# The 24 merge-gate tiles of a hybrid backbone layer, computed in pairs by Strassen's scheme after the RNN

## The chip, the cores and the metric

The kernel runs on one core of a Trainium2 chip. The metric is the device time of one execution in microseconds (us). The engines are TensorE (PE: matmuls; PEld: weight loads), VectorE (DVE), ScalarE (ACT), GpSimd (POOL) and SyncE (SP, which issues the DMAs). The kernel before takes 3270.88 us, the median of 3 runs (3266.74 to 3272.98).

## The reference

The reference runs two layers of a backbone over 1152 tokens, 1024 latent ones and 128 of a prompt, that share weights. D_MODEL is 1024. Cut to what matters here, one layer is:

```python
h = rmsnorm(x, g_norm) * (1 + scale) + shift            # scale, shift from a modulation matmul
parts = split(h @ w_in)                                  # x_rnn, g_rnn, c_q, c_kv, ..., merge_logits (3 x 1024)
xc = centred_conv(x_rnn, conv_w, conv_b)                 # 4 taps
r, i = sigmoid(xc @ w_a), sigmoid(xc @ w_i)              # block diagonal, 8 blocks of 128; forward and backward
a = exp(8 * r * log_sigmoid(lam))
u = sqrt(1 - a * a) * i * xc
y_rnn = scan(a, u) + reverse_scan(a, u)                  # h_t = a_t h_(t-1) + u_t
m = sigmoid(merge_logits)                                # three gates of 1024 channels per token
u = m0 * ((y_rnn * silu(g_rnn)) @ w_br_rnn) + m1 * (y_mla_gated @ w_br_mla) + m2 * (y_swa_gated @ w_br_swa)
x = x + gate * (u @ w_out)
```

The two attention branches (mla and swa) lie between the RNN and the last line and are not touched by the change. The columns of `w_in` that make `merge_logits` are 24 tiles of 128.

## The kernel before

All values are kept transposed, features on the 128 partitions and tokens along the free axis; the 1152 tokens are cut into 3 chunks of 384. Precision comes from splitting each operand into a high and a low half (`split`: ACT casts the high half, DVE or POOL subtracts it from the source) and issuing three matmuls per product of two 128-blocks (`mm3`: high by high, high by low, low by high). `H` holds the split normed input of a layer, one tile per chunk and half, 8 blocks of 128 features each. A weight tile of `w_in` is 128 output features by 1024 inputs: it is loaded by SP into one of three raw buffers (tag "wr"), split by ACT and POOL (`wload`) and used for three pieces of 24 matmuls, one per chunk.

The order of PE's instructions is the order of the program (`manual_schedule`); the order on the other engines is chosen by a scheduler from priorities and a model of time.

The first half of a layer is one block of code. `rnn_units(ft)` makes the 8 feature tiles of the RNN, each of 18 pieces: three x pieces (their evacuation into `xpad`; behind the last of them the convolution on DVE, L559 and L562, and the split into `xh` and `xl`), three g pieces (evacuated into `gsil`), and 12 gate pieces of 3 matmuls each, whose sigmoid is L587. Behind the last gate piece `scan()` runs on ACT, DVE and POOL (L600 to L622); it ends with the product in `gsil`, which SP stores as `yr` (L623). The buffers of a feature tile (`xpad`, `xc`, `xh`, `xl`, `gsil`, `r0`, `i0`, `r1`, `i1`, pool `rp`) exist once; `scan()` takes the buffers of `xh` and `xl` for its temporaries.

Between the RNN's pieces PE runs filler pieces from a list: eight feature-major tiles (silu gates of the two attention branches, 3 pieces each), five token-major tiles (9 pieces each) and the 24 merge-gate tiles (3 pieces each), 141 pieces. How many run behind which of the 18 pieces stands in

```python
RF = (0,) * 5 + (2,) + (1,) * 11 + (2,)
```

and `late_norm`, in the first feature tile of a layer, runs 4 more. Every third filler piece is followed by a step of the modulation matmuls (in layer 0 those left of layer 0 and all of layer 1; in layer 1 there are none). What is left of the list runs after the RNN, while four of the eight `yr` tiles are loaded back and split into the RNN's own buffers. A merge-gate piece is evacuated by a sigmoid on ACT (L728) and stored to `sg` in DRAM.

Then the merge of the RNN branch starts (`merge`, first unit `wide`, L855): it multiplies `w_br_rnn` with the 8 split `yr` tiles, takes the gates from `sg`, and interleaves the preparation of the mla branch. The other four `yr` tiles are loaded at its head. The rest of the layer (mla, swa, their merges, the output projection and the norm that makes the next layer's `H`) follows.

Of the kernel before, what the change touches and what calls it, by code (L numbers as in the profile page):

```python
# [9 lines left out]
F32 = mybir.dt.float32  # L10
# [16 lines left out]
RW = 1156  # L27
CTX = 1027
EPS = 1e-6
BIG = float(2.0 ** 100)  # L30
# [161 lines left out]
def _backbone(ctx, tc, nc, a, depth):  # L192
# [11 lines left out]
    def f(x):  # L204
        return x.bitcast(F32)
# [200 lines left out]

    def make_h(sp, hp, xt, rs, c, L, nm):
        hh = hp.tile([P, KT, CH], F32R, tag=f"h{c}", name=f"hh{nm}")
        hl = hp.tile([P, KT, CH], F32R, tag=f"l{c}", name=f"hl{nm}")
# [12 lines left out]
        return hh, hl  # L422

    hst = ExitStack()
    hp = pool("hp0", side="right", stack=hst)
    xp2 = pool("xp0", side="right", stack=hst)
    H = []
    with ExitStack() as ist:
# [32 lines left out]
        with tc.manual_schedule(engines={E.PE, E.Activation, E.DVE, E.Pool}):  # L461
# [29 lines left out]
            for c in range(2):  # L491
                H.append(make_h(sp, hp, [xts[c][:, k] for k in range(KT)], None, c, L, f"i{c}"))
        mod_units = mod_units[16:]

    for l in range(depth):
# [32 lines left out]

        rpst = ExitStack()
        with ExitStack() as rst:  # L530
            rp = pool(f"rnn{l}", stack=rpst)
            fp = pool(f"fw{l}", bufs=2, stack=rst)
            ep = pool(f"ev{l}", bufs=2, stack=rst)
            tp = pool(f"tm{l}", stack=rst)
            mdp = pool(f"md{l}", bufs=1, stack=rst)
            psr = pool(f"psr{l}", bufs=3, space=PSUM, stack=rst)
            rows = tp.tile([P, R_SINK], F32, name=f"rows{l}")
# [197 lines left out]
            mod_units = mod_units + more  # L735
            fill = []
            for i in range(5):
                if i == 4:
                    fill.append(tm_unit(i, tms[i]))
                if i < 4:  # L740
                    fill.append(in_unit("b", 16 + i, ev_silu(gm_d[i]), fp))
                    fill.append(in_unit("b", 20 + i, ev_silu(gs_d[:, i]), fp))
                    fill.append(tm_unit(i, tms[i]))
                if i == 3:
                    fill.append(in_unit("b", 24, ev_sig(sg_d[0]), fp))
            for m in range(1, 24):
                fill.append(in_unit("b", 24 + m, ev_sig(sg_d[m]), fp))

# [8 lines left out]
            def filler():  # L757
                if not G and count[0] == 4:
                    G.append(stream(mod_units))
                if next(F, G) is G:  # L760
                    return False
                count[0] += 1
                if count[0] % 3 == 0 and G:
                    next(G[0], None)
                return True

# [10 lines left out]
            def late_norm():  # L777
# [23 lines left out]
                for k in range(KT):  # L801
                    nc.vector.tensor_tensor(out=x2[k], in0=x2[k], in1=rs, op=ALU.mult)
                H.append(make_h(None, hp, x2, None, 2, L, f"i2_{l}"))
                filler()
# [3 lines left out]
            with tc.manual_schedule(engines={mybir.EngineType.PE}):  # L808
                for ft in range(8):
                    for _ in steps(ft):  # L810
                        pass
                    if ft == 1 and decay:
                        decay()
                ys = {}
                for g in range(2):
                    raw = xp2.tile([P, KT, 384], F32, tag="twl", name=f"yrb{l}_{g}").rearrange("p k n -> p (k n)")
                    for j in range(2):
                        k, y = 2 * g + j, raw[:, j * T:(j + 1) * T]
                        ys[k] = [rp.tile([P, T], F32R, tag=t, name=f"y{t}{l}_{k}")
                                 for t in (("r0", "r1"), ("i0", "i1"), ("xc", "xh"), ("xl", "gsil"))[k]]  # L820
# [6 lines left out]
                for _ in R:  # L827
                    pass

        hst.close()  # L830

# [48 lines left out]
        with ExitStack() as ast:  # L880
# [9 lines left out]
            with ExitStack() as yst:  # L890
                yrw = pool(f"yraw{l}", bufs=3, stack=yst)
                with tc.high_priority(offset=1500):
                    for i, k in enumerate((6, 7, 4, 5)):
                        if i < 3:
                            raw = yrw.tile([P, T], F32, tag="yr", name=f"yraw{l}_{k}")
                        else:
                            raw = rp.tile([P, XW], F32, tag="xpad", name=f"yraw{l}_{k}")[:, 0:T]
                        nc.sync.dma_start(out=raw, in_=yr_d[k])
                        split(ys[k][0], ys[k][1], raw, "act", "dve")

# [94 lines left out]

            M = stream(merge(ps6, "b", sp, "rnn", 8, a["w_br_rnn"][l], ys, 0, True, False, None, (0, 1, 2, 3, 6, 7, 4, 5)))
            groups = ([lambda g=g: ck_part(g) for g in range(0, 10, 2)] + [lambda: (kr_load(), [])[1]] +
# [19 lines left out]
            mst.close()  # L1017
            rpst.close()
            pso = pool(f"pso{l}", bufs=1, space=PSUM, stack=ast)
# [624 lines left out]
        xp2 = pool(f"xp{l + 1}", side="right", stack=hst)  # L1644
        UH = [hp.tile([P, KT, CH], F32R, tag=f"h{c}", name=f"uh{l}_{c}") for c in range(NCH)]
        UL = [hp.tile([P, KT, CH], F32R, tag=f"l{c}", name=f"ul{l}_{c}") for c in range(NCH)]
        psn = pool(f"psn{l}", bufs=1, space=PSUM, stack=fst)
# [89 lines left out]
        def cast(c):  # L1737
            rs = rstd_cast(fp, psn, "n", acc[c], f"y{l}_{c}")
            if not last:
                H2[c] = make_h(fp, hp, [xn[c][:, k] for k in range(KT)], rs, c, Ln, f"h{l}_{c}")  # L1740
                return
# [178 lines left out]
```

## Time and profile before

| what | value |
|---|---|
| median of 3 runs | 3270.88 us |
| the profiled execution's own time | 3271.47 us |
| its span (first to last instruction) | 3269.7 us |
| mean granted TensorE clock | 0.992 |
| PE busy | 3169.1 us (97%) |
| DVE, ACT, POOL busy | 1815.7, 1547.4, 1455.6 us (56%, 47%, 45%) |

The profile is of one execution. Busy PE time is made of matmuls whose records overlap, so the time that one matmul takes from its neighbours is read from starts or from counts in a stretch, not from the mean duration in a row. The RNN with its filler lies at about 50 to 902 us for layer 0 and 1660 to 2489 us for layer 1.

### The profile page before, as it was taken

What the parts mean: (1) busy time and instruction counts of PE and PEld (TensorE: products, weight loads), DVE (VectorE), ACT (ScalarE), POOL (GpSimd) and SP (SyncE); (2) the same over time, 40 slices, a digit from 0 to 9 for tenths busy, and PEclk for the clock granted to TensorE, in tenths of its full rate; (3) what the DMA queues carried; (4) which work ended last, traced back from release to release, by engine and by line L of the source; (5) the groups of instructions that cost most, each with busy time, mean ns of one, the idle gap of its engine ahead of it and who ended that gap; (6) DMA issues with size and microseconds to landing.
All of it is one profiled execution on the core that took longest, in us unless ns stands there. A gap on an engine that the chain in (4) does not pass through costs nothing. (4 is left out here: it accounts for less than half of the span.)

```text
span 3269.7 us, 52185 instructions
## 1 busy us (share of the span) xinstructions
PE 3169.1 (97%) x19572; PEld 3039.1 (93%) x19572; DVE 1815.7 (56%) x3253; ACT 1547.4 (47%) x3061; POOL 1455.6 (45%) x1174
## 2 busy tenths in 40 slices
PE   7999999999999999999999999999999999999998
PEld 4999999999999999898989999999999999989998
DVE  5345544322336888987572444433332388898766
ACT  3344444443315777764243433334342277786532
POOL 3655554443313444465374444333322144445643
PEclk9999999999999999999999999999999999999999
DMA  5333333333342102357533222222234400045564
GB/s 213 100 100 103 96 94 109 96 114 96 132 151 69 30 26 51 116 165 236 174 118 100 76 79 79 82 82 79 81 110 145 130 20 25 27 112 154 186 204 134
DMA packets 246652, 351.06 MB, mean 107 GB/s; under 512 B 73216, under 2 KB 200832, under 8 KB 246144
## 3 DMA queue, kind: packets, MB, share of 16 engines
q1 hardware_dynamic: 246400, 347.73, 34.1%
q8 instruction: 154, 2.52, 0.3%
q14 instruction: 98, 0.80, 0.1%
HBM read 248.87 MB, written 98.78 MB: 106 GB/s over the span
## 5 line engine op out<-in xcount | busy, mean ns | idle before, releaser
L239 PE MATMUL in<-hhi,wh_in 128*128 128x384 f32 x1536 | 519.8, 338 | 6.7 <-ACT osg L728 5.1
L239 PE MATMUL in<-hli,wh_in 128*128 128x384 f32 x1536 | 519.4, 338 | 2.2 <-DVE hli L421 2.1
L239 PE MATMUL in<-hhi,wl_in 128*128 128x384 f32 x1536 | 518.3, 337 | 0.0
L215 POOL TENSOR_TENSOR wl_in<-wr_in,wh_in 128x1024 fp32r<-128x1024 f32 x94 | 238.1, 2537 | 320.9 <-ACT wh_in L209 248.6
L239 PEld LDWEIGHTS in<-hhi,wh_in 128*128 128x128 f32 x1536 | 290.0, 189 | 7.6 <-ACT osg L728 5.8
L239 PEld LDWEIGHTS in<-hli,wh_in 128*128 128x128 f32 x1536 | 289.9, 189 | 4.7 <-DVE hli L421 4.7
L239 PEld LDWEIGHTS in<-hhi,wl_in 128*128 128x128 f32 x1536 | 290.0, 189 | 0.0
L239 PE MATMUL in<-hlh,wh_in 128*128 128x384 f32 x768 | 259.2, 337 | 2.3 <-DVE hlh L421 2.2
L239 PE MATMUL in<-hhh,wl_in 128*128 128x384 f32 x768 | 258.7, 337 | 2.1 <-POOL wl_in L215 2.1
L239 PE MATMUL in<-hhh,wh_in 128*128 128x384 f32 x768 | 258.7, 337 | 0.8 <-ACT osg L728 0.8
L1163 POOL TENSOR_SCALAR p<-p,mx 128x1152 f32<-128x1152 f32 x128 | 157.7, 1232 | 200.7 <-DVE mx L1160 124.3
L1214 DVE TENSOR_TENSOR pl<-pt,ph 128x512 fp32r<-128x512 f32 (+1 forms) x320 | 201.5, 637 | 27.9 <-ACT ph L1210 25.1
L1210 ACT CAST ph<-pt 128x512 fp32r<-128x512 f32 (+1 forms) x320 | 170.5, 551 | 91.5 <-PE pt L1203 87.0
L604 DVE SCALAR_TENSOR_TENSOR r<-r,txl 128x1156 f32<-128x1156 f32 x16 | 31.5, 1966 | 315.2 <-ACT r L603 315.2
L1203 PE MATMUL pt<-ident,p 128*128 128x128 f32 x1152 | 171.0, 274 | 9.8 <-DVE kl L1073 4.2
L728 ACT ACTIVATE osg<-in 128x384 f32<-128x384 f32 x144 | 68.9, 488 | 233.4 <-PE in L239 151.2
L1203 PEld LDWEIGHTS pt<-ident,p 128*128 128x128 f32 x1152 | 132.7, 140 | 34.4 <-DVE pl L1214 11.7
L209 ACT CAST wh_in<-wr_in 128x1024 fp32r<-128x1024 f32 x96 | 99.9, 1044 | 123.7 <-PE in L239 85.9
L1228 PE MATMUL o<-ph,v 128*128 128x256 f32 x576 | 153.0, 292 | 0.0
L239 PEld LDWEIGHTS in<-hlh,wh_in 128*128 128x128 f32 x768 | 144.4, 188 | 3.9 <-DVE hlh L421 3.9
L239 PEld LDWEIGHTS in<-hhh,wl_in 128*128 128x128 f32 x768 | 144.6, 188 | 2.4 <-POOL wl_in L215 2.4
L1228 PE MATMUL o<-pl,v 128*128 128x256 f32 x576 | 145.7, 280 | 0.0
(447 smaller groups left out, 9584.1 us busy)
## 6 DMA issues: line engine op xcount, KB each, us to landing
wr_in<-in_w_fm SPq DMA_DIRECT2D x96, 512.0 KB, 3.6
sg<-osg SPq DMA_DIRECT2D x144, 192.0 KB, 1.9
wr_wm<-in_w_mod SPq DMA_DIRECT2D x32, 512.0 KB, 4.1
wr_wo<-in_w_out SPq DMA_DIRECT2D x32, 512.0 KB, 3.7
yr<-gsil SPq DMA_DIRECT2D x16, 576.0 KB, 2.8
msgrnn<-sg SPq DMA_DIRECT2D x48, 192.0 KB, 2.4
u<-msgrnn SPq DMA_DIRECT2D x48, 192.0 KB, 2.6
qr<-qs SPq DMA_DIRECT2D x36, 256.0 KB, 4.0
```

The source lines that it names most:

```text
L209: nc.scalar.copy(out=hi, in_=src)
L215: eng.tensor_tensor(out=lo, in0=src, in1=f(hi), op=ALU.subtract)
L239: nc.tensor.matmul(ps, x, y, start=n == 0, stop=n == last)
L604: nc.vector.scalar_tensor_tensor(out=rr[d], in0=rr[d], scalar=1.0, in1=tt[d], op0=ALU.add, op1=ALU.mult)
L728: nc.scalar.activation(out=o, in_=ps, func=ACT.Sigmoid)
L1163: nc.gpsimd.tensor_scalar(out=pts[i], in0=pts[i], scalar1=mxs[i][:, 5:6], scalar2=1.0, op0=ALU.mult, op1=ALU.mult)
L1203: nc.tensor.transpose(ps[:, w:w + P], pts[q][:, k * P:(k + 1) * P], ident)
L1210: nc.scalar.copy(out=r["h", j][:, 0:width(j)], in_=r["t", j][:, 0:width(j)])
L1214: nc.vector.tensor_tensor(out=r["l", j][:, 0:width(j)], in0=r["t", j][:, 0:width(j)], in1=f(r["h", j][:, 0:width(j)]), op=ALU.subtract)
L1228: nc.tensor.matmul(O[:, 0:256], V[k][:, h % 4, :], x[:, 256 * i:256 * i + 256], start=k == 0 and e == 0, stop=k == 8 and e == 1)
```

## The change

The merge-gate tiles leave the filler list, whose order is written anew (69 pieces). `RF` and `steps` stay. `H` becomes two large tiles (`HB`, high and low), of which the chunks are slices.

After the RNN's pieces the pools of the RNN and the token-major tiles are closed, and three pairs of tiles `T1`, `T2`, `T4` (512 features by 576 tokens, in two halves) are opened in their memory. `H` is read as a 2 x 2 block matrix (`B11` to `B22`, 512 features by 576 tokens). `combine` makes `T1 = B12 - B11`, `T2 = B22 - T1`, `T4 = B21 - T2`, and `B22 - B12` in the place of `B12`. Two merge-gate weight tiles form the other 2 x 2 block matrix. For each of the 12 pairs seven products of 4 x 3 matmuls run over two column pieces (320 and 256), instead of 2 x 24 matmuls over each of three chunks of 384; sums of weight blocks are made on DVE and POOL (`sx`) and each weight block is split anew; sums of products are taken on evacuation by DVE, the sigmoid by ACT on 576 columns. A modulation step may follow a product as it followed a filler piece. At the head of the merge all eight `yr` tiles are loaded into tiles of their own, each raw into the tile of its low half.

```diff
+NH = 576
+SP = ((0, 0, 320), (512, 320, 576))
...
-            fill = []
-            for i in range(5):
-                if i == 4:
-                    fill.append(tm_unit(i, tms[i]))
-                if i < 4:
-                    fill.append(in_unit("b", 16 + i, ev_silu(gm_d[i]), fp))
-                    fill.append(in_unit("b", 20 + i, ev_silu(gs_d[:, i]), fp))
-                    fill.append(tm_unit(i, tms[i]))
-                if i == 3:
-                    fill.append(in_unit("b", 24, ev_sig(sg_d[0]), fp))
-            for m in range(1, 24):
-                fill.append(in_unit("b", 24 + m, ev_sig(sg_d[m]), fp))
+            gm = [in_unit("b", 16 + i, ev_silu(gm_d[i]), fp) for i in range(4)]
+            gs = [in_unit("b", 20 + i, ev_silu(gs_d[:, i]), fp) for i in range(4)]
+            tms = [tm_unit(i, ev) for i, ev in enumerate(tms)]
+            fill = [gm[0], gs[0], tms[0], gm[1], tms[1], gs[1], tms[2], gm[2], tms[3], gs[2], tms[4], gm[3], gs[3]]
...
-                ys = {}
-                for g in range(2):
-                    raw = xp2.tile([P, KT, 384], F32, tag="twl", name=f"yrb{l}_{g}").rearrange("p k n -> p (k n)")
-                    for j in range(2):
-                        k, y = 2 * g + j, raw[:, j * T:(j + 1) * T]
-                        ys[k] = [rp.tile([P, T], F32R, tag=t, name=f"y{t}{l}_{k}")
-                                 for t in (("r0", "r1"), ("i0", "i1"), ("xc", "xh"), ("xl", "gsil"))[k]]
-                        nc.sync.dma_start(out=y, in_=yr_d[k])
-                        split(*ys[k], y, "act", "dve")
+                for _ in R:
+                    pass
+                while count[0] < 63:
+                    filler()
+                tst.close()
+                stp = pool(f"st{l}", stack=rst)
+                TT = [[stp.tile([P, 4, NH], F32R, name=f"st{x}{l}_{i}") for x in "hl"] for i in range(3)]
+                sx = stp.tile([P, 4, P], F32, name=f"sx{l}")
+                et = xp2.tile([P, KT, CH], F32, tag="twl", name=f"et{l}").rearrange("p k n -> p (k n)")
+                slot = [et[:, i * NH:(i + 1) * NH] for i in range(5)]
+                quad = lambda i, j: [t[:, 4 * i:4 * i + 4, j * NH:(j + 1) * NH] for t in HB]
+                B11, B12, B21, B22 = quad(0, 0), quad(0, 1), quad(1, 0), quad(1, 1)
+                T1, T2, T4 = TT
+                nt = [0]
+
+                def combine(dst, a, b):
+                    for k in range(4):
+                        t = slot[nt[0] % 5]
+                        nt[0] += 1
+                        nc.gpsimd.tensor_tensor(out=t, in0=f(a[0][:, k]), in1=f(b[0][:, k]), op=ALU.subtract)
+                        nc.vector.tensor_tensor(out=t, in0=t, in1=f(a[1][:, k]), op=ALU.add)
+                        nc.vector.tensor_tensor(out=t, in0=t, in1=f(b[1][:, k]), op=ALU.subtract)
+                        split(dst[0][:, k], dst[1][:, k], t, "act", "dve")
+
+                combine(T1, B12, B11)
+                combine(T2, B22, T1)
+                combine(T4, B21, T2)
                 while filler():
+                    pass
+                combine(B12, B22, B12)
...
+                    def weights(i):
...
+                        src = (a11, sx, sx, a12, a21, sx, a22)[i]
+                        wq, t = ((wp, "w"), (fp, "f"))[nw[0] % 2]
+                        nw[0] += 1
+                        w = [wq.tile([P, 8, P], F32R, tag=t + x, name=f"ws{x}{l}_{m}_{i}")[:, 0:4] for x in "hl"]
+                        split(*w, src, "act", "pool")
+                        if i == 0:
+                            load(m + 2)
+                        if i == 6:
+                            load(m + 3)
+                        return w
+
+                    def product(i, w):
+                        b = (B11, T1, T2, B21, B12, B22, T4)[i]
+                        bank = pstp.tile([P, 1024], F32, tag="s", name=f"st{l}_{m}_{i}", bufs=3)
+                        for p0, c0, c1_ in SP:
+                            ps = bank[:, p0:p0 + c1_ - c0]
+                            for k in range(4):
+                                for z, (x, y) in enumerate(((0, 0), (0, 1), (1, 0))):
+                                    nc.tensor.matmul(ps, w[x][:, k], b[y][:, k, c0:c1_], start=k == 0 and z == 0, stop=k == 3 and z == 2)
+                            evac(i, ps, slice(c0, c1_))
+                        mod_step()
...
+                load(0)
+                load(1)
+                for _ in stream([u for m in range(0, 24, 2) for u in pair(m)], 3):
                     pass
...
-            for k in range(4, 8):
+            for k in (7, 6, 0, 1, 2, 3, 4, 5):
                 ys[k] = [yp.tile([P, T], F32R, name=f"y{x}{l}_{k}") for x in "hl"]
...
+            with tc.high_priority(offset=1500):
+                for k in range(8):
+                    raw = f(ys[k][1])
+                    nc.sync.dma_start(out=raw, in_=yr_d[k])
+                    split(ys[k][0], ys[k][1], raw, "act", "dve")
```

## Rows read from the trace of the kernel before

**Rows 1.** The page: busy time, share of the span and instructions of each engine.
```profile
PE 3169.1 (97%) x19572; PEld 3039.1 (93%) x19572; DVE 1815.7 (56%) x3253; ACT 1547.4 (47%) x3061; POOL 1455.6 (45%) x1174
```
**Rows 2.** Busy in one RNN turn: stretch, length, PE, PEld, DVE, ACT, POOL, clock, DMA.
```profile
556.00:654.50 98.50, 98.50 (x563) 95.95 (x562) 33.00 (x28) 40.94 (x58) 42.20 (x19) 1.00 0.32 99
```
**Rows 3.** DVE in time, 651 to 757 us: start, length, line, operation, [idle before].
```profile
654.36 0.88 DVE L559 TENSOR_SCALAR xc<-xpad,sv 128x1156 f32<-128x1156 f32 x1
655.27 4.34 DVE L562 SCALAR_TENSOR_TENSOR xc<-xpad,sv,xc 128x1156 f32<-128x1156 f32 x3
...
728.71 3.58 DVE L604 SCALAR_TENSOR_TENSOR r<-r,txl 128x1156 f32<-128x1156 f32 x1
...
734.88 1.36 DVE L606 SCALAR_TENSOR_TENSOR txl<-r 128x1156 f32<-128x1156 f32 x1
...
737.55 2.21 DVE L606 SCALAR_TENSOR_TENSOR txh<-r 128x1156 f32<-128x1156 f32 x1
...
748.68 2.43 DVE L620 TENSOR_TENSOR txh<-txh,txl 128x1155 f32<-128x1155 f32 x1 [0.35 <-POOL rg L618]
...
752.30 0.28 DVE L622 TENSOR_TENSOR gsil<-gsil,txh 128x128 f32<-128x128 f32 x1
```
**Rows 4.** ACT in time, 651 to 757 us.
```profile
659.70 1.16 ACT L209 CAST xh<-xc 128x1156 fp32r<-128x1156 f32 x1 [0.56 <-DVE xc L562]
...
723.35 0.59 ACT L587 ACTIVATE i<-g,sv 128x388 f32<-128x388 f32 x1
```
**Rows 5.** POOL in time, 651 to 757 us.
```profile
660.94 2.71 POOL L215 TENSOR_TENSOR xl<-xc,xh 128x1156 fp32r<-128x1156 f32 x1 [9.18 <-ACT xh L209]
...
728.67 2.41 POOL L215 TENSOR_TENSOR wl_in<-wr_in,wh_in 128x1024 fp32r<-128x1024 f32 x1
736.33 2.21 POOL L607 TENSOR_SCALAR r<-r 128x1156 f32<-128x1156 f32 x1 [5.25 <-DVE txl L606]
...
748.61 1.29 POOL L215 TENSOR_TENSOR wl_lru<-wr_lru,wh_lru 128x512 fp32r<-128x512 f32 x1
```
**Rows 6.** PE by line and shape, 870 to 900 us: count | busy, mean ns | idle.
```profile
L239 PE MATMUL in<-hhi,wh_in 128*128 128x384 f32 x58 | 19.6, 339 | 0.0
L239 PE MATMUL in<-hhi,wl_in 128*128 128x384 f32 x57 | 19.3, 339 | 0.0
L239 PE MATMUL in<-hli,wh_in 128*128 128x384 f32 x57 | 19.3, 339 | 0.0
```
**Rows 7.** PE in time: the first and last of 24 matmuls of a token-major piece.
```profile
484.92 0.28 PE L239 MATMUL tm<-twh,hhi 128*128 128x256 f32 x1
...
487.63 0.28 PE L239 MATMUL tm<-twh,hli 128*128 128x256 f32 x1
```
**Rows 8.** Groups by line and shape, whole span: count | busy, mean ns | idle, releaser.
```profile
L239 PE MATMUL in<-hhi,wh_in 128*128 128x384 f32 x1536 | 519.8, 338 | 6.7 <-ACT osg L728 5.1 <-ACT hhi L418 1.6
...
L587 ACT ACTIVATE r<-g,sv 128x384 f32<-128x384 f32 x64 | 37.1, 580 | 31.0 <-PE g L239 31.0
...
L868 DVE TENSOR_TENSOR msgrnn<-mgrnn,msgrnn 128x384 f32<-128x384 f32 x48 | 26.6, 557 | 118.0 <-PE mgrnn L239 103.7 <-PE mgrnn L855 9.5 <-DMA msgrnn<-sg 3.5
...
L215 POOL TENSOR_TENSOR twl<-twr,twh 128x576 fp32r<-128x576 f32 x8 | 11.3, 1433 | 1.0 <-ACT twh L209 0.9
...
L215 DVE TENSOR_TENSOR yl<-yraw,yh 128x1152 fp32r<-128x1152 f32 x8 | 10.3, 1352 | 88.3 <-ACT yh L209 88.3
```
**Rows 9.** PE in time, 73 to 76 us.
```profile
74.31 1.44 PE L789 MATMUL ssi<-ones,va 128*128 128x1 f32 x6 [4.08 <-DVE va L785]
```
**Rows 10.** Busy by stretch, as in rows 2, behind that wait.
```profile
75.00:80.00 5.00, 5.00 (x18) 5.00 (x19) 1.30 (x5) 0.00 (x0) 0.86 (x1) 0.50 0.02 3
```
**Rows 11.** The page: DMA issues, KB each, us from issue to landing.
```profile
wr_wm<-in_w_mod SPq DMA_DIRECT2D x32, 512.0 KB, 4.1
...
yr<-gsil SPq DMA_DIRECT2D x16, 576.0 KB, 2.8
```

More of the change, by code (lines that the diff above doesn't have):

```diff
@@ L425, in _backbone @@
     hp = pool("hp0", side="right", stack=hst)
+    HB = [hp.tile([P, KT, T], F32R, name=f"h{x}0") for x in "hl"]
     xp2 = pool("xp0", side="right", stack=hst)
@@ L491, in _backbone @@
             for c in range(2):
-                H.append(make_h(sp, hp, [xts[c][:, k] for k in range(KT)], None, c, L, f"i{c}"))
+                H.append(make_h(sp, HB, [xts[c][:, k] for k in range(KT)], None, c, L, f"i{c}"))
         mod_units = mod_units[16:]
@@ new lines, in pair, with evac @@
+                def pair(m):
+                    st = {}
+                    def weights(i):
+                        r0, r1 = raws[m], raws[m + 1]
+                        a11, a12, a21, a22 = r0[:, 0:4], r0[:, 4:8], r1[:, 0:4], r1[:, 4:8]
+                        if i == 1:
+                            nc.vector.tensor_tensor(out=sx, in0=a21, in1=a22, op=ALU.add)
+                        elif i == 2:
+                            nc.gpsimd.tensor_tensor(out=sx, in0=sx, in1=a11, op=ALU.subtract)
+                        elif i == 4:
+                            nc.vector.tensor_tensor(out=a21, in0=a11, in1=a21, op=ALU.subtract)
+                        elif i == 5:
+                            nc.gpsimd.tensor_tensor(out=sx, in0=a12, in1=sx, op=ALU.subtract)
+                        src = (a11, sx, sx, a12, a21, sx, a22)[i]
[17 more added lines that the diff above has]
+                            evac(i, ps, slice(c0, c1_))
+                        mod_step()
+                    def evac(i, ps, cs):
+                        add = lambda o, y: nc.vector.tensor_tensor(out=o[:, cs], in0=ps, in1=y[:, cs], op=ALU.add)
+                        if i == 0:
+                            nc.scalar.copy(out=c1[:, cs], in_=ps)
+                            return
+                        if i in (1, 2):
+                            if i == 2:
+                                add(u2, c1)
+                            add(xs, (c1, xs)[i - 1])
+                            return
+                        if cs.start == 0:
+                            st["o"] = slot[3 + no[0] % 2]
+                            no[0] += 1
+                        o = st["o"]
+                        add(o, (c1, xs, xs, u2)[i - 3])
+                        if i == 4:
+                            add(u2, u2)
+                        if cs.start:
+                            nc.scalar.activation(out=o, in_=o, func=ACT.Sigmoid)
+                            half = int(i in (4, 5))
+                            nc.sync.dma_start(out=sg_d[m + (i in (4, 6))][:, half * NH:(half + 1) * NH], in_=o)
+                    return [(lambda i=i: weights(i), [lambda w, i=i: product(i, w)]) for i in range(7)]
@@ L826, in _backbone @@
                     pass
-                for _ in R:
-                    pass
+        ys = {}
         hst.close()
@@ L1644, in _backbone @@
         xp2 = pool(f"xp{l + 1}", side="right", stack=hst)
-        UH = [hp.tile([P, KT, CH], F32R, tag=f"h{c}", name=f"uh{l}_{c}") for c in range(NCH)]
-        UL = [hp.tile([P, KT, CH], F32R, tag=f"l{c}", name=f"ul{l}_{c}") for c in range(NCH)]
+        HB = [hp.tile([P, KT, T], F32R, name=f"h{x}{l + 1}") for x in "hl"]
+        UH, UL = ([t[:, :, c * CH:(c + 1) * CH] for c in range(NCH)] for t in HB)
         psn = pool(f"psn{l}", bufs=1, space=PSUM, stack=fst)
@@ L1739, in cast @@
             if not last:
-                H2[c] = make_h(fp, hp, [xn[c][:, k] for k in range(KT)], rs, c, Ln, f"h{l}_{c}")
+                H2[c] = make_h(fp, HB, [xn[c][:, k] for k in range(KT)], rs, c, Ln, f"h{l}_{c}")
                 return
```

37 lines of the change are left out of this document (16 added, 21 removed).

## The prediction, made before the changed kernel was run

> **What bounds the kernel now.** I read the page's busy shares first. TensorE (PE) is busy 97% of the span and no other engine exceeds 56% [rows 1], so a saved matmul counts as long as its successor has data. Next I read one stretch per stage. Between two stores of yr (one feature tile of the RNN, 98.5 us) PE is busy for all of it at full clock, while DVE is busy 33 us, ACT 41 and POOL 42 [rows 2]. The reader is to see that the RNN stage, too, is set by PE, although each feature tile has a long serial part on DVE, ACT and POOL. That part is hidden by the filler pieces that the PE order puts between the RNN's own pieces. Then I read that serial part in time [rows 3 to 5], because the change takes filler away.
>
> **What the products save.** A piece's matmul with 384 columns: 58+57+57 = 172 in 30 us, 0.1744 us each [rows 6]. With 256 columns: from the first to the last of 24, 23 steps in 487.63-484.92 = 2.71 us, 0.1178 each [rows 7]. 320 columns lie between; by the slope (0.0566 over 128 columns) 0.1461. Per layer 24 tiles x 3 chunks x 24 = 1728 matmuls go, 301.4 us. There come 12 pairs x 7 products x 12 x 2 pieces = 2016, half of 320 and half of 256 columns, mean 0.1320: 266.1 us. Saved: 35.3 us per layer, 70.6 us in all, if PE is fed.
>
> In the steady stage it is. A product lasts 12 x (0.1461+0.1178) = 3.17 us, a pair 22.2. POOL has 7 low halves of 512 elements and two sums at 1.29 us each [rows 5], 11.6 us a pair. DVE has 16 additions out of PSUM, each under the 0.557 us of the 384-wide one [rows 8], and two sums, under 10.5 us. ACT has less. Weights are made three products (9.5 us) ahead. All hidden; without that cover a late split would cost 1 to 3 us per product.
>
> **What the removal of gate pieces uncovers.** This is the larger term. The list of filler shrinks from 141 pieces to 69 (24 of 384-column tiles, 45 of token-major ones), but the counts per step are as before: 15 per feature tile, and 4 more in the late norm of the first. So 19+15+15+15 = 64 are spent after four feature tiles, the last 5 fall in the fifth, and tiles 5, 6 and 7 (from 0) run with nothing between their own pieces. The two loops that would run filler after the RNN find none.
>
> Serial part of a feature tile: the last sigmoid of a gate ends at 723.35+0.59 = 723.94 and the last multiplication of the scan at 752.30+0.28 = 752.58, 28.6 us [rows 3, 4]. The next tile's convolution starts only behind it and takes 654.36 to 659.61, the cast of xh ends at 660.86, its low half at 663.65: 9.3 us [rows 3 to 5]. The gates read both, and xh and xl share buffers with the scan's temporaries, so no order can overlap the two. From the end of a tile's gates on PE to the next gates: 0.6 (the sigmoid) + 28.6 + 9.3 = 38.5 us. PE has for it only the next tile's six input pieces, 144 x 0.1744 = 25.1 us. Before, 15 filler pieces of about 4 us lay in it.
>
> Part of the 28.6 may go: L604 took 3.58 us, starting with a POOL weight split of 2.41 that began 0.04 us before it, and 1.36 is what such an instruction takes otherwise [rows 3, 5]; fewer splits, fewer such meetings. I take 2 us off: 36.4-25.1 = 11.3 us of idle PE before the gates of tiles 5, 6, 7, i.e. 34 us per layer. Bounds: 13.4 each with the chain as it stands; 9.3 each if none of L604, L606 (2.21 against 1.36) and L620 (2.43, beginning 0.07 us behind another POOL split, against 1.36) stood behind POOL, 4.1 us off, a chain of 24.5 [rows 3, 5].
>
> The gates themselves: 36 matmuls are 6.3 us of PE, 12 sigmoids of 0.58 are 7.0 on ACT [rows 8]. After 4.08 us in which PE waited, the granted clock was 0.50 from 75 to 80 us, 18 matmuls in 5 us, 0.278 each [rows 9, 10]; at that rate the 36 take 10 us. Between +0.7 and +3.7, I take +2.5 each, 7.5 per layer. The Trainium skill (TensorE: Matmul & The Clock Gate, "What's actually happening") has half rate as the default that activity releases, and agrees with the row; by it alone all three sets of gates run at half rate, 3.6 us per layer more than I take.
>
> **The handover to the products.** Behind the last gates PE has two products whose inputs exist (T1 can be made during the RNN, in memory free by then): 6.3 us. The third reads T2, whose high half lies over gsil. It is free when the last yr has landed, 2.8 us after issue [rows 11], and four casts and subtractions (0.68 us, half of the 1152-wide 1.352 [rows 8]) take 3.3: 0.6+26.6+0.1+2.8+3.3 = 33.4, less 6.3: 27.1 us idle. The fifth product needs the new B12, made on the same engines behind T4. A combination has 4 steps of one POOL subtraction (576 wide, 1.43) and three DVE operations (0.68). Do they run side by side? L606 took 1.36 us at 734.88 and 2.21 at 737.55; the second ended 1.2 us after the POOL instruction begun at 736.33 [rows 3, 5]: it stood behind POOL. One after the other a combination is 13.9 us, T4 and B12 27.8, less two products: 21.5 idle; side by side 16.4 and 10. I take 18. Handover: 45 us per layer (bounds 25, with B12 made early, and 51).
>
> SBUF — State Buffer in the Trainium skill ("Who interferes with whom") says that DVE instructions with two SBUF inputs and POOL exclude each other for a whole instruction. The L606 rows agree; by the rule the handover is 48.6, without it 37.1.
>
> **Small terms.** The merge now loads all eight y tiles into memory that the products leave; the last product frees the place of y4 and y5 and they are wanted 6 us into the merge, a load, cast and subtraction later: +2 per layer (0 to 6). The stalls in the gate tiles go (5.1 us behind osg over both layers [rows 8]): -3 per layer. In layer 0 the 18 steps of the modulation left after the RNN share three raw buffers with the pairs: +5. H as two large tiles: 0, since its readers and writers stand in the same order, and the next layer's first writes have the whole last stage as cover.
>
> **Sum.** Per layer 34+7.5+45+2-3 = 85.5 of new waits against 35.3 saved: +50.2; twice, and 5: +105. On the profiled execution's own 3271.5 (span 3269.7) that is 3376.9; the median of the runs shown lies 0.6 lower: **3376 us**. All low ends: per layer 28+2+25-3-35.3 = +16.7, so 3304. All high ends: 40+11+51+6-35.3 = +73 per layer and 40 for the modulation: 3457.
>
> **Rivals.**
> (a) Faster. The bare tiles close up: with filler work gone from ACT, DVE and POOL the chain of a tile shrinks to what PE does meanwhile. Place: the gates of tiles 5 to 7. It decides from a chain of about 28 us between two sets of gates (break-even: 35 of waits per layer, of which the handover keeps 27). Then only the handover stays: 3271-71+2x27 = 3254. For it: ACT and POOL are half idle [rows 2]. Against: from L604 to L622 DVE works 752.58-728.71 = 23.9 us, some 20 without POOL in its way, and convolution, cast and low half follow serially [rows 3 to 5]. 6%.
> (b) Lighter. The chain falls to its shortest instructions and the new B12 is made early: 3278 to 3335, middle 3305. For it: the order on those engines is free. Against: the locks with POOL that are the scan's own (L607) stay. 15%.
> (c) The products starve in layer 0: a modulation weight waits for a raw buffer until a pair's fifth weight is made, then needs 4.1 us for its load, a cast and 2.41 for its low half [rows 5, 11], against 9.5 of lead. At 5 us for each of some 14 units: +70, 3446. 13%.
>
> **How the numbers follow.** The main case, 3335 to 3425, has 63%; (a) 6%; (b) 15%; (c) and all high ends 13%; the rest (3%) lies within 0.2%, 6.5 us, which is about what a measurement here can tell from no change. The range for 8 in 10 takes the main case, most of (b) and the lower part of (c): 3300 to 3445. Faster 0.06, same 0.03, slower 0.91.
>
> **What would show it.** Right: yr stores of tiles 5 to 7 come every 43 to 47 us, not 98; PE idle 9 to 13 us before each of those gates, ended by xh or xl; after the last gates two products, 25 to 30 us idle, two products, 5 to 20 us idle; then 80 products at 3.2 us. Wrong: no idle before those gates (a); matmuls of 256 columns at 0.17 us, so that the products save nothing; idle PE before modulation matmuls throughout the pairs (c). If PE's total busy time does not fall by about 70 us, the first step fails.

## The result, and the profile after

The changed kernel takes 3689.06 us (median of 4 runs, 3685.14 to 3692.32), the kernel before 3271.93 (4 runs beside it): a ratio of 1.1278, interval 1.1258 to 1.1297. Slower, as forecast, but by 417 us and not by 105; the prediction's range ended at 3445. The merge begins 214 us later in layer 0 and takes 201 us more to come in layer 1; the rest of the two kernels differs by less than 6 us. The page's busy line, which answers to [rows 1]:

```profile
PE 3187.0 (86%) x20148; PEld 3006.7 (81%) x20148; DVE 2107.3 (57%) x3781; ACT 1623.5 (44%) x3199; POOL 1691.8 (46%) x1374
```

PE has 18 us more of busy time, not 70 less, and 97% have become 86%. The stretches (columns as in [rows 2]) are a bare tile twice, the handover, and 200 us of the product stage in layer 1:

```profile
560.00:608.00 48.00, 33.51 (x182) 33.20 (x182) 29.94 (x22) 23.85 (x33) 21.50 (x11) 0.86 0.12 40
608.00:655.00 47.00, 31.95 (x169) 31.32 (x169) 28.88 (x22) 23.20 (x32) 20.48 (x11) 0.85 0.10 36
656.00:727.00 71.00, 0.80 (x3) 0.40 (x3) 67.86 (x57) 18.95 (x26) 37.53 (x22) 0.50 0.04 16
2600.00:2800.00 200.00, 165.87 (x1162) 153.31 (x1163) 56.60 (x124) 51.62 (x89) 80.02 (x62) 1.00 0.22 76
```

In the last one, where I had PE fed, it is busy 166 us of 200 with the clock at full speed: 200/1162 = 0.1721 us per matmul against the 0.1320 of the prediction, 4.13 us per product against 3.17. PE in time, two products of that stretch, in each the last matmuls of the 320-column piece and the first of the 256-column one:

```profile
2702.28 0.31 PE L881 MATMUL st<-stl,wsh 128*128 128x320 f32 x1
2702.42 0.31 PE L881 MATMUL st<-sth,wsl 128*128 128x320 f32 x1
2703.37 0.38 PE L881 MATMUL st<-sth,wsh 128*128 128x256 f32 x1 [0.64 <-DVE et L886]
2703.59 0.28 PE L881 MATMUL st<-stl,wsh 128*128 128x256 f32 x1
2703.71 0.28 PE L881 MATMUL st<-sth,wsl 128*128 128x256 f32 x1
...
2706.45 0.30 PE L881 MATMUL st<-sth,wsl 128*128 128x320 f32 x1
2707.74 0.39 PE L881 MATMUL st<-sth,wsh 128*128 128x256 f32 x1 [0.98 <-DVE et L886]
```

and DVE at the same time:

```profile
2702.82 0.49 DVE L886 TENSOR_TENSOR et<-st,et 128x320 f32<-128x320 f32 x1 [5.35 <-PE st L881]
2705.10 0.42 DVE L886 TENSOR_TENSOR et<-st,et 128x256 f32<-128x256 f32 x1 [1.78 <-PE st L881]
2706.79 0.89 DVE L886 TENSOR_TENSOR et<-st,et 128x320 f32<-128x320 f32 x2 [1.27 <-PE st L881]
```

The pitches are those predicted (0.147 and 0.117 us from start to start), and between two products PE does not stop. But ahead of the second piece it stands until DVE has read the first out of PSUM: 0.64 us for one addition, 0.98 for two. Both pieces are slices of one tile, `bank`. The summary of waits says the same (engine, for whom, us, times, longest):

```profile
PE st L881 <- ACT et L888: 151.9, 24, 70.3
...
PE st L881 <- DVE et L886: 110.6, 144, 2.5
```

The 151.9 us are 24 times the second piece of a pair's first product; two of these waits are the handover and make up 140.5 us. PE in time ahead of the gates of tile 6, at the handover, and ahead of the merge:

```profile
596.49 0.69 PE L241 MATMUL g<-xh,wh_lru 128*128 128x384 f32 x1 [14.49 <-DVE gsil L576]
...
653.89 0.41 PE L881 MATMUL st<-hh,wsh 128*128 128x320 f32 x1 [2.01 <-ACT i L589]
726.69 0.58 PE L881 MATMUL st<-hh,wsh 128*128 128x256 f32 x1 [70.20 <-ACT et L888]
...
1116.27 0.69 PE L942 MATMUL mgrnn<-yh,wh_rnn 128*128 128x384 f32 x1 [5.77 <-ACT yh L211]
```

Summed over PE's records from the first input piece of a layer to its merge, in us above the kernel before:

| | predicted, per layer | layer 0 | layer 1 |
|---|---|---|---|
| PE waits ahead of gates | 34 | 56.5 | 58.4 |
| gates' own time (half clock) | 7.5 | 8.0 | 8.4 |
| handover to the products | 45 | 72.2 | 70.4 |
| other waits within the products | 0 | 62.6 | 61.0 |
| products' own time less that of the gate tiles | -35.3 | -4.6 | -5.6 |
| modulation | 5 (layer 0) | 14.4 | 0 |
| ahead of the merge | 2 | 5.8 | 5.7 |

The rest (token-major pieces, other input pieces, the stalls counted at -3) sums to -1 and 3. The fifth row isn't -35 because some 85 waits cost at their edges too: the matmul ahead of one counts to its own end (0.31 us, where the pitch is 0.147; 13 us per layer), and the one behind it takes 0.22 us to the next start, the others 0.117 (9 us). Besides, the products next to the handover begin at the lower level of the clock (granted: 0.50 over the wait, 0.73 from 727 to 733 us).

### The profile page after: what moved, and what is told of

It reads as the page before. It is cut to its first block, busy times and chain, and to the rows that moved or that the text cites. A ratio compares the mean times of both kernels' runs of the same rounds, so it can differ in the third digit from the quotient of the medians.

```text
span 3690.5 us, 54522 instructions
## 1 busy us (share of the span) xinstructions
PE 3187.0 (86%) x20148; PEld 3006.7 (81%) x20148; DVE 2107.3 (57%) x3781; ACT 1623.5 (44%) x3199; POOL 1691.8 (46%) x1374
## 5 line engine op out<-in xcount | busy, mean ns | idle before, releaser
L881 PE MATMUL st<-hh,wsh 128*128 128x320 f32 (+1 forms) x768 | 239.5, 312 | 211.9 <-ACT et L888 151.9
L241 PE MATMUL in<-hl,wh_in 128*128 128x384 f32 x1152 | 393.4, 342 | 7.9 <-DVE hl L422 7.9
L241 PE MATMUL in<-hh,wh_in 128*128 128x384 f32 x1152 | 393.1, 341 | 4.7 <-ACT xpad L556 3.0
L241 PE MATMUL in<-hh,wl_in 128*128 128x384 f32 x1152 | 391.5, 340 | 2.1 <-POOL wl_in L217 2.1
L241 PEld LDWEIGHTS in<-hl,wh_in 128*128 128x128 f32 x1152 | 219.9, 191 | 12.6 <-DVE hl L422 12.6
L881 PE MATMUL st<-hh,wsl 128*128 128x320 f32 (+1 forms) x768 | 228.6, 298 | 0.0
L881 PE MATMUL st<-hl,wsh 128*128 128x320 f32 (+1 forms) x768 | 228.6, 298 | 0.0
L241 PEld LDWEIGHTS in<-hh,wh_in 128*128 128x128 f32 x1152 | 220.2, 191 | 5.1 <-ACT xpad L556 3.3
L241 PEld LDWEIGHTS in<-hh,wl_in 128*128 128x128 f32 x1152 | 219.8, 191 | 2.4 <-POOL wl_in L217 2.4
L241 PE MATMUL tm<-twh,hh 128*128 128x256 f32 (+2 forms) x720 | 215.8, 300 | 0.0
```

The costliest lines, as they stand in the source:

```text
L241: nc.tensor.matmul(ps, x, y, start=n == 0, stop=n == last)
L881: nc.tensor.matmul(ps, w[x][:, k], b[y][:, k, c0:c1_], start=k == 0 and z == 0, stop=k == 3 and z == 2)
```

## The experiments

All are compared with the kernel before on the same chip.

**Two PSUM tiles (e1).** Theory: the framework orders the matmuls of the second piece behind the reading of the first since both are one tile. Rival: DVE is late.

```diff
-    bank = pstp.tile([P, 1024], F32, tag="s", ..., bufs=3)
...
-        ps = bank[:, p0:p0 + c1_ - c0]
+        ps = pstp.tile([P, 512], F32, tag=f"s{p0}", ..., bufs=3)[:, 0:c1_ - c0]
```

> The two column pieces of a product (320 and 256) get a PSUM tile each, in the same six banks; nothing else changes. Theory A (the second piece waits for the evacuation of the first because both are slices of one tile): in the changed kernel PE idles 0.64 to 0.98 us before nearly every 256-wide piece, and in layer 1 82 products take 347 us where 3.17 us each make 260. With two tiles that idle time goes: 70 to 90 us per layer, 3510 to 3550 us in all, and the product pace becomes 3.2 to 3.4 us. Theory B (evacuation or weights cannot keep the pace, whatever the tiles): the idle time moves to another place in the product and the time stays above 3640 us.

Measured 3517.61, ratio 1.0745: 171 us gone. The product stage of layer 1 by stretch, and DVE at one product of it:

```profile
2500.00:2700.00 200.00, 200.00 (x1518) 200.00 (x1517) 82.06 (x162) 68.07 (x119) 105.50 (x82) 1.00 0.29 102
```
```profile
2602.59 0.49 DVE L885 TENSOR_TENSOR et<-st,et 128x320 f32<-128x320 f32 x1 [4.55 <-PE st L880]
```

PE is full: 200/1518 = 0.1318 us per matmul, the prediction's 0.1320. The reading takes 0.49 us as before, now beside the second piece, whose first matmul started at 2602.34.

**One tile, read once both pieces are written (e2).** If the tile is what matters and not its memory, the order alone does it.

```diff
             for k in range(4):
...
-            evac(i, ps, slice(c0, c1_))
+        for p0, c0, c1_ in SP:
+            evac(i, bank[:, p0:p0 + c1_ - c0], slice(c0, c1_))
```

> One PSUM tile as in the changed kernel, but both pieces are written before either is evacuated. Theory A: no read of the tile stands between the two pieces any more, so the wait inside the product goes as with two tiles, 3510 to 3560 us; the ring of three tiles still covers the evacuation. Theory B: a later evacuation makes it worse, 3690 us or more.

Measured 3517.87 (1.0746), the same; 1518 matmuls in the same 200 us. So the memory was never the limit, nor DVE: it was a reading placed between two writes of one tile. The Trainium skill (PSUM — Partial Sum Buffer, "Summary: rules for kernel authors") lets an engine read PSUM beside a matmul in another bank; e1 agrees, 0 us of wait where there were 0.64 to 0.98.

**The combinations keep off slot 0 (e3).** The 70.2 us end with the evacuation of product 0 into `slot[0]`, which the combinations also use.

```diff
-    t = slot[nt[0] % 5]
+    t = slot[3 + nt[0] % 2]
```

> The combinations use only the last two of the five temporaries, so the three that hold sums of products (c1, xs, u2) are free from the start. Theory H1 (the single 70 us wait behind the first half product is the evacuation of c1, which must not overwrite a temporary before the last combination): the first product is evacuated at once and the 70 us split into waits for T1, T2 and the new B12; products 0 to 3 (about 12 us) run inside them, 20 to 28 us less in all, 3660 to 3670. Rival H2 (PE would have waited for T1 and T2 anyway and two temporaries make the combinations slower): no gain, 3685 to 3710.

Measured 3674.78 (1.1226): 14 us, less than the 20 to 28 expected. PE in time, three of the waits into which the one falls:

```profile
673.16 0.63 PE L881 MATMUL st<-sth,wsh 128*128 128x320 f32 x1 [17.37 <-ACT wsh L211]
...
685.39 0.63 PE L881 MATMUL st<-sth,wsh 128*128 128x320 f32 x1 [3.43 <-ACT sth L211]
...
732.23 0.58 PE L881 MATMUL st<-hh,wsh 128*128 128x256 f32 x1 [20.29 <-DVE et L886]
```

The shared slot only gathered the waits; the products move into them, but the work that they wait for is as long. The waits of the product stage fall by 27 us over both layers, and its matmuls last 24 us longer beside the new waits. So the handover gave 3 of the 14 us; some 13 stand ahead of the gates of tile 4 (8.1 us of wait become 1.8, 8.9 become 2.5), for which the edit was not meant. The last of the three waits is again for a shared slot: product 3 is evacuated into `slot[3]`, which the combinations now use.

**The same filler spread over all tiles, mostly among the gate pieces (e4).**

```diff
-RF = (0,) * 5 + (2,) + (1,) * 11 + (2,)
+RF = (0,) * 5 + (1,) + (1, 0) * 5 + (1,) + (1,)
```

> Eight filler pieces per RNN feature tile in place of 15 (nine in the first), so that the 69 pieces last through the eighth tile. Theory: the waits before the gates of tiles 4 to 7 (8.1, 14.5, 14.5, 13.0 us in layer 0) and the half-rate gates behind them go, some 55 us per layer, 3575 to 3590 us; stores of yr come every 60 to 70 us in all tiles. Rival (the chain of a tile is longer than PE's own work plus eight pieces, about 60 us, so every tile now waits a little): 3620 us or more.

Measured 3690.58 (1.1274): nothing. The waits ahead of the gates are smaller but in nearly every tile (64.5 and 57.3 us per layer, 60.7 and 67.0 in the kernel after; PE in time, tile 4), and yr comes every 65 to 74 us:

```profile
404.50 0.69 PE L241 MATMUL g<-xh,wh_lru 128*128 128x384 f32 x1 [10.00 <-DVE gsil L576]
```

Filler between the gate pieces puts the scan off; only what stands between the last gate piece of a tile and the first of the next covers it, and of the 8 pieces that is two.

**The filler between the x and g pieces (e5, with e1).** 8 pieces in each tile, fewer ahead of the gates of the first, where the late norm runs four.

```diff
-RF = (0,) * 5 + (2,) + (1,) * 11 + (2,)
+RF = (1,) * 5 + (2,) + (0,) * 11 + (1,)
...
-                    for _ in range(2 if ft == 0 and i == 5 else RF[i]):
+                    for _ in range((2 if i == 5 else 0) if ft == 0 and i < 6 else RF[i]):
...
-                while count[0] < 63:
+                while count[0] < 69:
```

> The two PSUM tiles of the run with 3517.6 us, and beside them the 69 pieces of filler spread evenly: 8 for each feature tile, six of them between the x and g pieces, one behind them and one behind the gates, and none left for the handover. Theory: the waits ahead of the gates of the bare feature tiles (8.1, 14.5, 14.5 and 13.0 us in layer 0) and the gates at half the clock are due to having no filler between the x and g pieces; both go, about 52 + 9 us per layer. But the six pieces that ran in the kernel after behind the last gates (about 25 us) no longer cover the last scan, so the wait at the handover grows by about 25. Sum: 3517 - 2*(61 - 25) = 3445, range 3425 to 3465. Rival, that the RNN's own chain on DVE sets the period wherever the filler stands (as the run with filler among the gate pieces seemed to say): at or above 3517.

Measured 3366.8 (1.0282): 151 us below e1, twice what I expected. Groups over the whole span, in the kernel after and in this one (columns as in [rows 8]), and a stretch of two tiles here:

```profile
L241 PE MATMUL g<-xh,wh_lru 128*128 128x384 f32 (+1 forms) x192 | 72.9, 380 | 114.3 <-DVE gsil L576 101.7 <-ACT xh L211 12.6
```
```profile
L241 PE MATMUL g<-xh,wh_lru 128*128 128x384 f32 (+1 forms) x192 | 68.3, 356 | 17.7 <-ACT r L589 9.0 <-ACT xh L211 6.4 <-DVE gsil L576 2.0
```
```profile
411.00:536.00 125.00, 122.92 (x808) 120.06 (x807) 79.75 (x111) 56.37 (x81) 85.40 (x52) 1.00 0.30 94
```

The waits ahead of the gates go, and so does the half clock. My expectation was wrong about the rest: in the kernel after no filler runs behind the last gates (the 69 are spent in the fifth tile, as the prediction had it); here the counts leave six, which cover the last scan. The first wait of the handover falls from 25.5 us in e1 to 6.0, and does not grow by 25. So the 151 us have two parts: some 115 ahead of the gates and in them, 39 at the handover.

**Thirteen pieces kept for the handover (e6, with e1 and e3).** 7 in each tile; the order of the list is changed so that the token-major pieces come early enough.

```diff
+RF = (1,) * 6 + (0,) * 11 + (1,)
...
-    fill = [gm[0], gs[0], tms[0], gm[1], tms[1], gs[1], tms[2], ..., gm[3], gs[3]]
+    fill = [gm[0], gs[0], tms[0], a1, tms[1], a2, tms[2], a3, tms[3], b1, tms[4], b2, gm[2], gs[2], gm[3], gs[3]]
...
-                while count[0] < 63:
-                    filler()
```
(`a1` to `a3` are the three pieces of `gm[1]`, `b1` and `b2` those of `gs[1]`.)

> As the even placement with two PSUM tiles, but only 7 pieces of filler for each feature tile (56), with 13 silu-gate pieces (about 55 us) kept for behind the last gates, where the last scan (about 23 us) and the combinations of H's blocks (about 46 us of DVE) run; combinations use the two slots that no product needs first, and the PSUM of the filler is given back after it. Theory: the waits ahead of the gates go (61 us per layer) and of the 63 us of waits at the handover some 20 stay (23 + 46 + 7 for the filler's own DVE work - 55): 3517 - 2*(61 + 43) = 3309, range 3275 to 3330. Rival, that the combinations are held up behind the filler's evacuations or the filler behind them, so that the handover's waits stay: 3395 or more.

Measured 3331.45 (1.0179), 1 us above the range. The 63 us of waits at the handover are 15 and 18, the longest in layer 0:

```profile
626.70 0.58 PE L891 MATMUL st<-hh,wsh 128*128 128x256 f32 x1 [7.50 <-DVE osl L724]
```

16.3 and 5.6 us came up ahead of token-major pieces, whose weights are made late in the new order; I had not counted them.

**All of a combination on DVE (e7, with e1).**

```diff
-    nc.gpsimd.tensor_tensor(out=t, in0=f(a[0][:, k]), in1=f(b[0][:, k]), op=ALU.subtract)
+    nc.vector.tensor_tensor(out=t, in0=f(a[0][:, k]), in1=f(b[0][:, k]), op=ALU.subtract)
```

> Two PSUM tiles, and the first subtraction of each combination on DVE instead of POOL (16 per layer). In the kernel after a DVE operation of the combinations takes 0.75 us alone and 1.8 to 1.95 us while POOL works. Theory, that the two engines hold each other up: 64 operations at 0.75 us and no hand-over between the engines are some 10 us per layer shorter, 3490 to 3510. Rival, that four operations at 0.75 us are no shorter than three at a mean of 1.0: 3515 to 3535.

Measured 3505.24 (1.0711): 12 us less than e1, with 16 more operations on DVE per layer. DVE in e1 and in this run:

```profile
685.46 1.81 DVE L217 TENSOR_TENSOR stl<-et,sth 128x576 fp32r<-128x576 f32 x1
687.20 1.81 DVE L831 TENSOR_TENSOR et<-et,hl 128x576 f32<-128x576 f32 x1
688.93 1.95 DVE L832 TENSOR_TENSOR et<-et,stl 128x576 f32<-128x576 f32 x1
```
```profile
693.91 0.75 DVE L830 TENSOR_TENSOR et<-hh,sth 128x576 f32<-128x576 f32 x1
694.58 0.75 DVE L832 TENSOR_TENSOR et<-et,stl 128x576 f32<-128x576 f32 x1
695.25 0.75 DVE L217 TENSOR_TENSOR stl<-et,sth 128x576 fp32r<-128x576 f32 x1
```

**The combinations left out (e8, with e1).** It prices them.

```diff
-                combine(T1, B12, B11)
...
-    b = (B11, T1, T2, B21, B12, B22, T4)[i]
+    b = (B11, B12, B22, B21, B12, B22, B21)[i]
```

> Two PSUM tiles, and the four combinations of H's blocks (T1, T2, T4 and B22 - B12) left out: each product reads a block of H in their place, so the sums of H's blocks are not computed. It prices the handover. Theory, that the handover's waits (25.5 + 5.3 + 4.2 + 4.1 + 2.4 + 21.4 = 63 us per layer) are the combinations': about 3517 - 2*63 = 3392, up to 3420 if the last scan still holds up the evacuation of the first products on DVE. Rival, that the handover waits for the last scan and for the memory of the RNN whatever is computed: 3480 or more.

The gates then come from other sums than the reference's. Measured 3407.33 (1.041): 55 us per layer, of which 38 are waits at the handover, 7 the matmuls beside them, and 8 to 9 a wait ahead of the gates of tile 4. One wait of the handover stays, that of product 1, whose weight sum runs on DVE right behind the last scan:

```profile
664.17 0.64 PE L874 MATMUL st<-hh,wsh 128*128 128x320 f32 x1 [24.09 <-ACT wsh L211]
```

**A buffer of its own for the modulation's raw weights in the product stage (e9, on e6).** In the memory that the RNN leaves.

```diff
+    raw = st["raw"].tile([P, 512], F32, tag="mraw", ..., bufs=1)
+    nc.sync.dma_start(out=raw, in_=a["w_mod"][l, c, q][:, k, :])
+    split(hi[:, k], lo[:, k], raw, "act", "pool")
```

> The covered kernel (3331 us), and in the product stage the raw weights of the modulation in a buffer of their own (in two halves of 256 KB) instead of the three buffers that they share with the raw gate weights. In the covered kernel PE waits 18.1 us in layer 0 ahead of modulation matmuls, of which there were 1.0 us in the kernel before. Theory, that a pair of gate tiles holds the shared raw buffers for its seven products and the modulation's load waits for them: 3331 - 15 = 3316. Rival, that ACT and POOL, which split these weights beside those of the products, are late: no change, 3325 to 3335.

Measured 3318.77 (1.0143): 12.7 us. Among the products the waits ahead of modulation matmuls fall from 16.2 us to 0.4, so the shared buffers were their cause. But 24 us of such waits come up ahead of the first product, most of them in one (PE in time), and the waits of the first products in layer 0 fall from 15.0 to 2.6 us in exchange:

```profile
583.87 0.59 PE L316 MATMUL mod<-wh_wm,sc 128*4 128x512 f32 x1 [17.34 <-ACT wh_wm L211]
```

**Four gate tiles as filler again (e10, on e9).** With the order of filler of the kernel after.

```diff
+    sg = [in_unit('b', 24 + i, ev_sig(sg_d[i]), fp) for i in range(4)]
+    fill = [gm[0], gs[0], tms[0], ..., gm[3], gs[3]] + sg
...
-    for m in range(0, 24, 2) for u in pair(m)
+    for m in range(4, 24, 2) for u in pair(m)
```

> The run with the modulation's own buffer, and four of the 24 gate tiles computed as in the kernel before, by 12 pieces of filler behind the others, and the order of the filler as in the kernel after: 63 pieces (8 for each feature tile) in the RNN, 18 (about 75 us) behind it over the last scan and the combinations; the other 20 tiles in ten pairs. Theory, that what is left above the kernel before is waits at places without cover: the 16.3 and 5.6 us ahead of token-major pieces go, of the 15.0 and 17.8 us ahead of the first products about 23 go, and the four tiles cost 12*4.18 - 14*3.17 = 5.9 us per layer more: 3316 - 22 - 23 + 12 = 3283, range 3265 to 3300. Rival, that the combinations are as slow beside the filler's evacuations as the filler is long, so that the waits only move: 3310 or more.

Measured 3280.49, ratio 1.0025 (1.0015 to 1.0035). Within 3 us of the sum. Ahead of products PE waits 0.0 and 2.6 us; what is left in layer 0 stands ahead of the modulation:

```profile
597.36 0.59 PE L316 MATMUL mod<-wh_wm,sc 128*4 128x512 f32 x1 [7.69 <-ACT wh_wm L211]
...
602.27 0.59 PE L316 MATMUL mod<-wh_wm,sc 128*4 128x512 f32 x1 [2.93 <-ACT wh_wm L211]
```

**That buffer only behind the filler (e11, on e10).**

```diff
+                L["st"]["raw"] = stp     # moved behind "while filler(): pass"
```

> The hybrid (3280.5 us), with the modulation's own raw buffer used only behind the filler: it lies in the memory of the RNN, and in the hybrid PE waits 7.7 + 2.9 + 2.6 + 1.8 + 2.4 = 17.4 us ahead of modulation matmuls between 589 and 638 us of layer 0, while the last scan still holds that memory. Theory, that those loads wait for the RNN's memory: 3280.5 - 12 = 3268, range 3263 to 3273, as long as before. Rival, that the splits of these weights on ACT and POOL are late there whatever buffer they come from: 3278 to 3283.

Measured 3269.04, ratio 0.9992 (0.998 to 1.0003). The group of that line (as in [rows 8]; those of the low halves still wait some 5 us in layer 0):

```profile
L316 PE MATMUL mod<-wh_wm,sc 128*4 128x512 f32 x64 | 25.2, 394 | 0.0
```

**Another order of the products (e12, on e11).**

```diff
-    return [... for i in range(7)]
+    return [... for i in (0, 1, 2, 4, 6, 3, 5)]
```

> The same, and in each pair the products in the order 0, 1, 2, 4, 6, 3, 5 instead of 0 to 6 (the same products and sums), so that the last two read blocks of H and not T1, T2, T4. PE waits 5.37 us (layer 0) and 4.41 us (layer 1) ahead of the first matmul of the merge, released by ACT's split of the RNN output, which is loaded into the memory of T1, T2, T4. Theory, that the wait is for the last product that reads T4: that memory is free 6.3 us earlier, and 8 us go in both layers: 3268 - 8 = 3260, range 3255 to 3266, faster than before. Rival, that the load waits for H or for the transfers of the last gates: no change against the run with the late buffer.

Measured 3267.95, ratio 0.9989 (0.9981 to 0.9998). The wait at the merge stands as it was (4.61 us in e11, 4.25 here), so the memory of T4 is not what it is for. The trace points elsewhere: the last matmul that reads T4 starts at 887.79 us, and the y loads are issued 5 us later, right behind two stores of gates, the second of which waits for a sigmoid that ends on ACT at 892.83. That their place in SP's order holds them is not shown, since no run moves them. PE at the merge, and SP ahead of it:

```profile
898.63 0.69 PE L961 MATMUL mgrnn<-yh,wh_rnn 128*128 128x384 f32 x1 [4.25 <-ACT yh L211]
```
```profile
889.32 3.86 SPq L924 DMA_DIRECT2D sg<-et  x2
893.27 4.33 SPq L999 DMA_DIRECT2D yl<-yr  x8
```

## Why the prediction was wrong

**The step that failed: "In the steady stage it is", and at its end "All hidden".** I compared the work of DVE, POOL and ACT in a pair with its length, and it does fit. I did not ask in what order a product's own steps must follow. With a reading of `bank` between its two pieces, the reading is on PE's path: 62.6 and 61.0 us of waits, and 30 and 24 us more for the matmuls (296.2 and 290.1 us against 266.1). That is some 178 of the 313 us by which the time was missed, the half clock next to the handover included. e1 and e2, which take that order away in two ways, give 171 back (17 of it in shorter waits at the handover), and then the product takes 24 x 0.1318 = 3.16 us. So "Saved: 35.3 us per layer" was right for a fed PE, and PE was not fed. The sign that the prediction gave for this step, PE's busy time down by about 70 us, does not tell the two apart: in e1, at the predicted pitch, it is 3155.6 us, down by 14, since gates and products beside the waits that are left last longer.

**The bare tiles were mis-sized: 41.5 us per layer with the gates, 64.5 and 66.8 measured.** Tiles 5 to 7 wait 14.50, 14.49 and 13.04 us, not 11.3, and tile 4 waits 8.1: of its five filler pieces I had not asked how many stand ahead of its gates, and that is two. Tiles 2 and 3 wait 3.0 and 3.7 us. From the last gate matmul of tile 5 to the first of tile 6, PE, DVE, ACT and POOL show what came late (compare [rows 3 to 5]):

```profile
556.71 0.34 PE L241 MATMUL g<-xh,wl_lru 128*128 128x388 f32 x1
```
```profile
591.86 0.28 DVE L624 TENSOR_TENSOR gsil<-gsil,txh 128x128 f32<-128x128 f32 x1
595.88 1.48 DVE L576 TENSOR_TENSOR gsil<-gsil,in 128x384 f32<-128x384 f32 x3 [3.75 <-ACT gsil L575]
```
```profile
559.12 0.58 ACT L589 ACTIVATE i<-g,sv 128x388 f32<-128x388 f32 x1
...
592.23 1.16 ACT L211 CAST xh<-xc 128x1156 fp32r<-128x1156 f32 x1 [9.27 <-DVE gsil L624]
...
595.36 1.26 ACT L575 ACTIVATE gsil<-in 128x384 f32<-128x384 f32 x3 [0.68 <-DMA yr<-gsil]
```
```profile
593.46 2.62 POOL L217 TENSOR_TENSOR xl<-xc,xh 128x1156 fp32r<-128x1156 f32 x1 [5.21 <-ACT xh L211]
```

The last sigmoid ends at 559.70, 2.7 us behind the last gate matmul (557.05) and not 0.6: a tanh and a weight cast stand before it on ACT. The kernel before had this too: the sigmoid that [rows 4] shows ends 2.6 us behind that tile's last gate matmul:

```profile
720.98 0.34 PE L239 MATMUL g<-xh,wl_lru 128*128 128x388 f32 x1
```

These 2 us per tile the chain lacked. From the sigmoid to the end of xl it took 36.4 us, 35.9 forecast, though the convolution, which I had behind the scan, partly ran inside it. The gates start at 596.49, released by `gsil`: the g pieces can't be evacuated until the yr store has landed out of the one `gsil`, and their PSUM buffers are those of the gates. But xl, which the second gate matmul reads, is there only at 596.08, so this wait cost 0.4 us here (at most 1.1, in tile 6 of layer 1). The half rate of the gates (8.0 and 8.4 us for 7.5) came near. e4 and e5 show the cause: where the filler stands, not how much there is.

**The handover: 45 forecast, 72.2 and 70.4 measured.** e1, where it no longer is one wait, shows two of about the sizes that I gave (27.1 and 18), but in other places and for other reasons, so that the sizes were luck: PE in time,

```profile
679.90 0.64 PE L880 MATMUL st<-sth,wsh 128*128 128x320 f32 x1 [25.51 <-ACT wsh L211]
686.06 0.63 PE L880 MATMUL st<-sth,wsl 128*128 128x320 f32 x1 [5.25 <-POOL wsl L217]
...
731.54 0.63 PE L880 MATMUL st<-hh,wsh 128*128 128x320 f32 x1 [21.35 <-ACT et L887]
```

DVE and ACT ahead of the first and the last of them:

```profile
678.31 0.28 DVE L624 TENSOR_TENSOR gsil<-gsil,txh 128x128 f32<-128x128 f32 x1
678.51 0.68 DVE L856 TENSOR_TENSOR sx<-wr_in 128x512 f32<-128x512 f32 x1
```
```profile
731.06 0.70 ACT L887 COPY et<-st 128x320 f32<-128x320 f32 x2 [0.83 <-DVE hl L217]
```

I had two products behind the last gates and the third waiting for T2, whose memory `gsil` holds. Only product 0 runs: product 1 waits 25.5 us for the weight sum `sx`, which comes on DVE right behind the last scan, and T1's low halves follow it there. e8 computes no T2 and keeps this wait, at 24.1 us. The second long wait is not the fifth product's for the new B12 but the fourth's: its PSUM tile (there are three) is that of product 0, which goes into `slot[0]` only when the last combination has left that. Not forecast were 16 us within products 1 and 2, where weight sums and the combinations share DVE and POOL, and in the kernel after the same slot, which with one PSUM tile stopped PE in the middle of product 0. Of the two cases that I weighed for DVE beside POOL, "one after the other" is the one that happened: 0.75 us alone, 1.81 to 1.95 with POOL. The rule that the prediction took from SBUF — State Buffer in the Trainium skill ("Who interferes with whom") agrees with this, and e7 with it.

**Small terms.** The merge waits 5.8 and 5.7 us (2 forecast). The stalls counted at -3 did not go: ahead of input pieces PE waits 6.5 and 8.1 us, before 5.9 and 8.3. The modulation cost 14.4 us in layer 0 (5 forecast): rival (c) had the mechanism, shared raw buffers, and e9 shows it among the products, but at a fifth of its price. Rivals (a) and (b) did not happen.

**The sum.** The runs from e5 to e12 undo the costs in turn; e11 and e12, with 20 of 24 tiles still in pairs, arrive at 3269 and 3268 us. That is as long as before within 0.2%, with the interval of e12 just below 1. PE's time for products falls as computed (222.6 and 222.1 us for 1680 matmuls), 57 us in all. In e11's trace some 34 us of new waits and 11 us of pieces that last longer stand against it.

## What to carry to other kernels

Throughput that fits does not show that a step is hidden: for each buffer, write down in which order its writes and reads must follow, and look for a read between two writes of one tile; two tiles cost nothing and were worth 171 us here. When work is taken out of a stage, ask what it was covering and where the rest of it stands: the same 69 pieces, moved ahead of the place where the serial chain ends, with six kept for the handover, were worth 151 us, and among the gates nothing. A shared temporary turns several short waits into one long one, which hides how many causes there are.

## What the runs showed of the hardware beside this

A matmul of 256 columns that follows a wait of 0.64 to 0.98 us takes 0.22 us to the next start, the others 0.117, though the granted clock is 1.00 in that stretch. With a wait of 13.0 to 14.5 us in it, a bare tile had a mean granted clock of 0.85 to 0.86; over the wait of 70.2 us it was 0.50, the lower of the two levels (1.2 GHz), and from 727 to 733 us, behind that wait, 0.73. The first matmuls after these waits took 0.69 (384 columns) and 0.58 us (256).
